# TensorE in source order in the tails, and the last joint projection token tile by token tile

## The chip, the cores and the metric

The kernel runs on one core of a Trainium2 chip. The metric is the device time of one execution in microseconds (us). The median of three runs before the change is 2194.53 us (2194.24 to 2195.38). TensorE, VectorE, ScalarE, GpSimd and SyncE are written PE, DVE, ACT, POOL and SP in the profile's rows. SP issues the loads of weights.

## What is computed

A backbone of two layers over 256 latent tokens and 256 context tokens of width 1024. Each layer is a half-step SwiGLU FFN, a mixer and a second half-step FFN; every one of the three normalises its input, shifts and scales it, and adds its normalised and gated output to the stream:

```python
def rmsnorm(x, w):
    xf = x.astype(jnp.float32)
    y = xf * lax.rsqrt(jnp.mean(xf * xf, axis=-1, keepdims=True) + EPS)
    return (y * w.astype(jnp.float32)).astype(x.dtype)

def modulate(x, g, shift, scale):
    return rmsnorm(x, g) * (1.0 + scale) + shift

def add_residual(x, y, g_post, gate, weight):
    return x + weight * gate * rmsnorm(y, g_post)

def swiglu(h, w_in, w_out):
    a, b = jnp.split(h @ w_in, 2, axis=-1)
    return (jax.nn.silu(a) * b) @ w_out

def branch_merge(ret_out, diff_out, gates, w_out):
    g_a, g_b = jnp.split(jax.nn.sigmoid(gates), 2, axis=-1)
    return (g_a * ret_out + g_b * diff_out) @ w_out
```

The mixer is a retention branch and a differential-attention branch from one input projection; `branch_merge` is its joint output projection. In the last layer only the latent tokens need an output, so the last joint projection and the last FFN work on 256 tokens. The FFN's inner width is 2816.

## The kernel before

The stream lies in SBUF as four token tiles X[0] to X[3] of 128 tokens x 1024, 0 and 1 latent, 2 and 3 context. Every product is taken three times (`mm3`, L330 to L332) on operands split into a hi and a lo part. Weights come from HBM in pieces of 512 KB (`load`, L147), through four raw buffers; `split` writes the hi part on ScalarE (L154) and the lo part on VectorE (L155), into five `w` buffers. Smaller operands live in a ring of twenty slots (`slot`, "r" in the rows), VectorE's scratch in `t` tiles.

An FFN has 22 steps of the first product (`fin_mm`: 128 gate and 128 value columns over eight k), each followed by SiLU and a product, and then the second product over 11 pairs of hidden tiles. In the last FFN, a step of the first product is 48 matmuls of 256 columns.

An FFN and a joint projection end in a **tail**. The first pairs or pieces are worked off for all token tiles; what is left is done one token tile after the other, 12 matmuls for each half of 512 columns, so 24 a tile. Behind a tile's second half `post_norm(t)` follows: two Squares with a sum on ScalarE (L317), the products with the gate row on VectorE (L319), the reciprocal root in three steps on GpSimd (`rstd_2`, L254 to L257) and the residual steps on VectorE (L325). After token tile 1 `after()` is called: `norm_pair(LAT)` normalises X[0] and X[1] (`norm_xn`: L267 on ScalarE, `rstd_2`, L270 on VectorE), transposes them on TensorE (16 transposes, L280), scales and shifts them on ScalarE (eight times L289) and splits them into `h` on VectorE (L292, L293), for the first product of the next stage. The scheduler chooses where in TensorE's order those transposes stand, as for everything. There are four tails with four token tiles: the FFN and the mixer of layer 0, its second FFN and the first FFN of layer 1.

In the last layer the **last joint** has two token tiles. `wide(9)` and `wide(7)` are the last parts of the input projection; `ev_gA(1)` merges the branches (tanh on ScalarE L852, two steps on VectorE L853 and L854, four transposes L861 a token tile, copied and split at L863 and L864) into `M[0, t]` and `M[1, t]`. Then three of the four `wout` pairs are worked off for both tiles as they come, the last for each tile apart, and `norm_pair(LAT)` and the last FFN follow. Loads of `cc` and `wada` (L163, L170) feed the gate rows and have been placed between the others on SP's queue.

Of the kernel before, what the change touches and what calls it, by code (L numbers as in the profile page):

```python
# [12 lines left out]
F32R = mybir.dt.float32r  # L13
# [5 lines left out]
P = 128  # L19
# [15 lines left out]
def build(ctx, tc, a):  # L35
# [84 lines left out]
    def small(n, tag):  # L120
        return sm.tile([P, n], F32, tag=tag, name=tag)
# [125 lines left out]
    def chain(*gs):  # L247
        for g in gs:
            for _ in g:
                yield  # L250

    def rstd_2(ss):
        m = small(2, "pm")
        pool.tensor_scalar(out=m[:, 0:1], in0=ss[:, 0:1], scalar1=1.0 / D, scalar2=EPS, op0=ALU.mult, op1=ALU.add)  # L254
        pool.tensor_scalar(out=m[:, 1:2], in0=ss[:, 1:2], scalar1=1.0 / D, scalar2=m[:, 0:1], op0=ALU.mult, op1=ALU.add)
        r = small(1, "pr")
        pool.tensor_tensor(out=r, in0=m[:, 1:2], in1=cneg[:, 0:1], op=ALU.pow)  # L257
        return r

    def norm_xn(c, alloc):  # L260
        xs = []
        for j in range(2):
            t = 2 * c + j
            ss = small(2, "ss")
            for hf in range(2):
                junk = jp.tile([P, 512], BF16, tag="ja", name="ja")
                act(junk, X[t][:, hf * 512:(hf + 1) * 512], AF.Square, accum_out=ss[:, hf:hf + 1])  # L267
            r = rstd_2(ss)
            xn = alloc([P, D])
            dve.tensor_scalar(out=xn, in0=X[t], scalar1=r, scalar2=None, op0=ALU.mult)  # L270
            xs.append(xn)
        return xs

    def norm_t(c, q, xs):
        bk = bank()
# [30 lines left out]
    def start(AB):  # L306
        h = new_h()
        norm_pair(LAT, AB, h)
        return h, None

    def post_norm(t, yb, Gb, out=None):
        c = t // 2
        ss = small(2, "ss")
        us = []
        for hf in range(2):
            junk = jp.tile([P, 512], BF16, tag="ja", name="ja")
            act(junk, yb[hf], AF.Square, accum_out=ss[:, hf:hf + 1])  # L317
            u = tmp2()
            dve.tensor_tensor(out=u, in0=yb[hf], in1=Gb[c][:, hf * 512:(hf + 1) * 512], op=ALU.mult)  # L319
            us.append(u)  # L320
            banks.put(yb[hf])
        r = rstd_2(ss)
        for hf in range(2):
            xs = X[t][:, hf * 512:(hf + 1) * 512]
            dve.scalar_tensor_tensor(out=xs, in0=us[hf], scalar=r, in1=xs, op0=ALU.mult, op1=ALU.add)  # L325
            if out is not None:
                nc.sync.dma_start(out[t][:, hf * 512:(hf + 1) * 512], xs)

    def mm3(o, wH, wL, xH, xL, start, stop):
        mm(o, lhsT=wH, rhs=xH, start=start, stop=False)  # L330
        mm(o, lhsT=wH, rhs=xL, start=False, stop=False)  # L331
        mm(o, lhsT=wL, rhs=xH, start=False, stop=stop)  # L332

    early = {}
# [18 lines left out]
    def ffn(l, i, st, AB, fetch, pairs, side, nside, after=None, out=None):  # L353
        h, begun = st

        def fin_mm(fs, ws, abs_, c0, c1):
# [11 lines left out]
            banks.put(*ab)  # L368

        f0 = 0  # L370
        if begun is not None:
            f0 = len(begun)
            for f in range(f0):
                fin_ev(f, begun[f])
        elif len(pairs) == 2:
            w01 = [fin_w(l, i, 0), fin_w(l, i, 1)]
            ab01 = [[bank(), bank()], [bank(), bank()]]
            fin_mm((0, 1), w01, ab01, 0, 256)
            xs = norm_xn(CTX, tmp4)
# [14 lines left out]
            done[1] = want  # L394

        for f in range(f0, NF):
            w = fin_w(l, i, f, pin=len(pairs) == 1 and f < 2)
# [36 lines left out]
            pass  # L434
        slots.put(*cs.values())
        cs.clear()
        tail = [fout_w(NP - 2), fout_w(NP - 1)]
        if i == 1 and l < L - 1:
            fin_early(l + 1, 0, ((0, 0),))
        Gb = fetch()  # L440
        for t in range(NT):
            for hf in range(2):
                for e in range(2):
                    for j in range(2):
                        fout_mm(t, j, tail[e][0], tail[e][1], False, e == 1 and j == 1, (hf,))
            post_norm(t, y[t], Gb, out)
            if t == 1 and after is not None:
                after()
        slots.put(*tail[0][1], *tail[1][1], *Gb.values())

    def mixer(l, st, AB, fetch, after):
        h = st[0]
        last = l == L - 1
        lam_init = 0.8 - 0.6 * math.exp(-0.3 * l)
# [519 lines left out]
        fin_early(l, 1, ((0, 0), (0, 1), (1, 0))[:1 if NQ == 2 else 3])  # L974
        Gb = fetch()
        for t in range(NT):
            for hf in range(2):
                for k in range(2 * n0, 8):
                    wo_mm(t, k, w[k - 2 * n0], False, k == 7, (hf,))
            post_norm(t, yb[t], Gb)  # L980
            if t == 1:
                after()
        slots.put(*M.values(), *Gb.values())

    def startup():
        A = small(16, "adaA").rearrange("p (c k) -> p c k", c=2)
# [97 lines left out]
        nc.sync.dma_start(dtab, a["dtab"])  # L1084
        return AB, (h, abs_)

    AB, st0 = startup()
    box = [st0]
    for l in range(L):
        last = l == L - 1  # L1090
        g0, F0 = ada_gate(l, 0, 0.5)
        gs1, AB1 = ada_shsc(l, 1)
        g1, F1 = ada_gate(l, 1, 1.0)
        gs2, AB2 = ada_shsc(l, 2)
        ffn(l, 0, box.pop(), AB, F0, (LAT, CTX), chain(g0, gs1, g1, gs2), 24,
            after=lambda: box.append(start(AB1)))
        mixer(l, box.pop(), AB1, F1, after=lambda: box.append(start(AB2)))
        g2, F2 = ada_gate(l, 2, 0.5)
        if last:
            ffn(l, 1, box.pop(), AB2, F2, (LAT,), g2, 5, out=a["out"])  # L1100
        else:
            gs, AB = ada_shsc(l + 1, 0)
            ffn(l, 1, box.pop(), AB2, F2, (LAT, CTX), chain(g2, gs), 13, after=lambda: box.append(start(AB)))


def rope_tables():
# [64 lines left out]
```

## Time and profile before

| | |
|---|---|
| median of three runs | 2194.53 us (2194.24 to 2195.38) |
| the profiled execution | 2194.1 us, its span 2192.3 us |
| mean granted TensorE clock | 0.996 |
| TensorE busy | 2140.4 us, 98% |
| VectorE, ScalarE, GpSimd busy | 1365.7, 865.8, 129.1 us |
| DMA | 306.99 MB, mean 140 GB/s |

A matmul of 512 columns shows as 0.39 us, but one starts every 0.227 us, since they overlap in the array. So an idle time in brackets counts from the end that is drawn for the matmul before, and a loss is better read from starts. The granted clock is a share of 2.4 GHz; 0.50 is 1.2 GHz.

### The profile page before, as it was taken

Reading aid. Unit: us, or ns where it says so; the run is one execution under the profiler, and the core shown is the slowest. Engines: PE = TensorE matmul, PEld = TensorE weight load, DVE = VectorE, ACT = ScalarE, POOL = GpSimd, SP = SyncE. Lnnn points to the kernel's source line nnn. Section 1 sums busy time; section 2 is a strip of 40 time slices with the busy share of each in tenths; the row PEclk is TensorE's granted clock in tenths of the full one; section 3 lists DMA queues with packets and bytes.
Section 4 is the critical chain, followed back from the end, with each engine's and each line's share of the span. In section 5 each row is a group of like instructions: output and inputs, shape, how many; then the busy total and the mean of one; then the engine's idle time right before and its main releaser. Section 6 shows DMA issues by size and latency. Waiting matters only on the chain. (4 is left out here: it accounts for less than half of the span.)

```text
span 2192.3 us, 27590 instructions
## 1 busy us (share of the span) xinstructions
PE 2140.4 (98%) x10730; PEld 1790.6 (82%) x10730; DVE 1365.7 (62%) x2108; ACT 865.8 (39%) x1367; POOL 129.1 (6%) x236
## 2 busy tenths in 40 slices
PE   7999999999999999999999999999999999998998
PEld 5888888778788878888888888888878888878997
DVE  4799372678665774596243279825347776787554
ACT  3322332553533553522232242223245544565453
POOL 1000000201010000200000010000010000001000
PEclk9999999999999999999999999999999999999999
DMA  8866342222122234364334247734323323355554
GB/s 332 284 218 217 106 135 96 88 68 85 51 91 98 68 97 148 132 211 155 97 124 139 91 161 224 269 96 134 97 67 109 115 93 108 123 194 174 187 183 134
DMA packets 85060, 306.99 MB, mean 140 GB/s; under 512 B 9968, under 2 KB 10048, under 8 KB 84928
## 3 DMA queue, kind: packets, MB, share of 16 engines
q1 hardware_dynamic: 81936, 296.78, 41.2%
q0 software_dynamic: 2848, 8.43, 1.4%
q8 instruction: 84, 1.38, 0.3%
q14 instruction: 48, 0.39, 0.1%
q10 hardware_dynamic: 144, 0.01, 0.0%
HBM read 304.10 MB, written 1.09 MB: 139 GB/s over the span
## 5 line engine op out<-in xcount | busy, mean ns | idle before, releaser
L155 DVE TENSOR_TENSOR w<-raw,w 128x1024 fp32r<-128x1024 f32 x408 | 497.2, 1222 | 465.6 <-ACT w L154 461.9
L154 ACT CAST w<-raw 128x1024 fp32r<-128x1024 f32 x408 | 427.5, 1053 | 665.4 <-PE ps L332 609.3
L330 PE MATMUL ps<-h,w 128*128 128x512 f32 (+1 forms) x1868 | 664.7, 357 | 4.7 <-ACT w L154 2.6
L331 PE MATMUL ps<-h,w 128*128 128x512 f32 (+1 forms) x1868 | 664.9, 356 | 0.4 <-DVE h L293 0.3
L332 PE MATMUL ps<-h,w 128*128 128x512 f32 (+1 forms) x1868 | 663.6, 356 | 1.2 <-DVE w L155 1.2
L330 PEld LDWEIGHTS ps<-h,w 128*128 128x128 f32 x1868 | 353.4, 190 | 57.2 <-DVE h L292 4.7
L332 PEld LDWEIGHTS ps<-h,w 128*128 128x128 f32 x1868 | 353.8, 190 | 50.6 <-DVE w L155 1.8
L331 PEld LDWEIGHTS ps<-h,w 128*128 128x128 f32 x1868 | 354.1, 190 | 50.2 <-DVE h L293 1.4
L174 DVE CUSTOM_DVE_ANT_0 jd<-r,r 128x1024 bf16<-128x1024 f32 x224 | 273.4, 1221 | 6.8 <-DMA r<-wada_dram 2.0
L330 PE MATMUL ps<-w,h 128*128 128x512 f32 x544 | 216.1, 398 | 15.5 <-ACT r L577 11.9
L331 PE MATMUL ps<-w,h 128*128 128x512 f32 x544 | 214.3, 394 | 0.0
L332 PE MATMUL ps<-w,h 128*128 128x512 f32 x544 | 213.8, 394 | 0.0
L330 PE MATMUL ps<-w,gs 128*128 128x512 f32 x504 | 196.2, 389 | 0.0
L331 PE MATMUL ps<-w,gs 128*128 128x512 f32 x504 | 196.1, 389 | 0.0
L332 PE MATMUL ps<-w,gs 128*128 128x512 f32 x504 | 196.1, 389 | 0.0
L366 ACT ACTIVATE t<-ps 128x512 f32<-128x512 f32 (+1 forms) x88 | 47.9, 545 | 252.0 <-PE ps L332 250.6
L330 PEld LDWEIGHTS ps<-w,h 128*128 128x128 f32 x544 | 102.7, 189 | 38.2 <-ACT r L577 15.2
L367 DVE TENSOR_TENSOR r<-ps,t 128x512 f32<-128x512 f32 (+1 forms) x88 | 54.8, 622 | 105.3 <-PE ps L332 77.7
L331 PEld LDWEIGHTS ps<-w,h 128*128 128x128 f32 x544 | 102.8, 189 | 20.2 <-DVE w L155 1.5
L332 PEld LDWEIGHTS ps<-w,h 128*128 128x128 f32 x544 | 102.5, 188 | 20.4
L330 PEld LDWEIGHTS ps<-w,gs 128*128 128x128 f32 x504 | 94.6, 188 | 19.8
L332 PEld LDWEIGHTS ps<-w,gs 128*128 128x128 f32 x504 | 94.6, 188 | 19.6
(180 smaller groups left out, 2132.8 us busy)
## 6 DMA issues: line engine op xcount, KB each, us to landing
raw<-fin_dram SPq DMA_DIRECT2D x176, 512.0 KB, 4.3
r<-wada_dram SPq DMA_DIRECT2D x144, 512.0 KB, 5.1
raw<-fout_dram SPq DMA_DIRECT2D x88, 512.0 KB, 3.6
raw<-winW_dram SPq DMA_DIRECT2D x80, 512.0 KB, 3.6
raw<-winT_dram SPq DMA_DIRECT2D x48, 512.0 KB, 3.6
raw<-wout_dram SPq DMA_DIRECT2D x16, 512.0 KB, 5.6
r<-scr POOLq DMA_DIRECT2D x10, 512.0 KB, 5.4
r<-cc_dram SPq DMA_DIRECT2D x7, 512.0 KB, 5.2
```

Source lines behind the costliest of these rows:

```text
L154: keep(nc.scalar.copy(w[:, 0, :], src))
L155: keep(dve.tensor_tensor(out=w[:, 1, :], in0=src, in1=w[:, 0, :], op=ALU.subtract))
L174: dve.tensor_tensor_reduce(out=junk, in0=r[j], in1=cs[c], scale=1.0, scalar=0.0, op0=ALU.mult, op1=ALU.add, accum_out=out[:, c, 2 * u + j: ...
L330: mm(o, lhsT=wH, rhs=xH, start=start, stop=False)
L331: mm(o, lhsT=wH, rhs=xL, start=False, stop=False)
L332: mm(o, lhsT=wL, rhs=xH, start=False, stop=stop)
L366: act(sg[:, :N], ab[0][:, :N], AF.Silu)
L367: dve.tensor_tensor(out=g[f // 2][:, f % 2, :N], in0=ab[1][:, :N], in1=sg[:, :N], op=ALU.mult)
```

## The change

It has three parts. **Tails**: a function `tail` puts TensorE in source order (`manual_schedule`), and in the source the latent transposes now stand between the two halves of token tile 3; the normed tiles are made by `norm_x` right behind `post_norm` of tiles 0 and 1. **Last joint**: `last_joint` loads and splits all eight `wout` pieces at the start (four into the slot ring by `split2`, four into `w`), does token tile 0 completely, then tile 1, with the norm of tile 0 (`norm_tile`) inside; `head(0)` does three FFN steps for tile 0 alone while the norm of tile 1 is made, and `head(1)` the same for tile 1. Its products have the tokens as stationary operand, so six transposes bring the gated tiles into the FFN's layout; the FFN then starts with its fourth step. `cc` and `wada` loads come later on SP's queue, as slots are short. **Norms**: `rstd_2` takes one GpSimd step less (the Square is scaled by 1/32, so the two sums are added in one step), and the norm of the input is one Square over 1024 columns.

```diff
     def rstd_2(ss):
-        m = small(2, "pm")
-        pool.tensor_scalar(out=m[:, 0:1], in0=ss[:, 0:1], scalar1=1.0 / D, scalar2=EPS, op0=ALU.mult, op1=ALU.add)
-        pool.tensor_scalar(out=m[:, 1:2], in0=ss[:, 1:2], scalar1=1.0 / D, scalar2=m[:, 0:1], op0=ALU.mult, op1=ALU.add)
+        m = small(1, "pm")
+        pool.tensor_scalar(out=m, in0=ss[:, 0:1], scalar1=ss[:, 1:2], scalar2=EPS, op0=ALU.add, op1=ALU.add)
...
+    def norm_x(t, alloc):
+        ss = small(1, "sx")
+        junk = jp.tile([P, D], BF16, tag="ja", name="ja")
+        act(junk, X[t], AF.Square, scale=1.0 / 32, accum_out=ss)
...
+    def tail(NT, part, finish, AB):
+        xs = []
+        with tc.manual_schedule(engines={nc.tensor.engine}):
+            for t in range(NT):
+                part(t, 0)
+                if t == 3 and AB is not None:
+                    h = new_h()
+                    for q in range(4):
+                        norm_q(LAT, q, xs, AB, h)
+                part(t, 1)
+                finish(t)
+                if t < 2 and AB is not None:
+                    xs.append(norm_x(t, tmp4))
+        return None if AB is None else (h, None)
...
+    def last_joint(l, M, fetch, AB):
+        low, high, fw, owned = [], [], [], []
+        for u in range(4):
+            for r in load(a["wout"][l, u]):
+                if u < 2:
+                    wv, w = split2(r)
+                    low.append(wv)
+                    owned += w
+                else:
+                    w = split(r)
+                    high.append([w[:, 0], w[:, 1]])
...
+        for f in range(2):
+            for j in range(2):
+                fw_tile(f, j, f == 0 and j == 0)
+        Gb = fetch()
...
+        with tc.manual_schedule(engines={nc.tensor.engine}):
             for hf in range(2):
+                part(0, range(8), hf)
+            post_norm(0, yb[0], Gb)
+            xs = [norm_x(0, tmp4)]
+            for hf in range(2):
+                part(1, range(4), hf)
+            slots.put(*owned)
+            for j in range(2):
+                fw_tile(2, j, False)
+            part(1, range(4, 8), 0)
+            norm_tile(0, xs[0], AB, h)
+            part(1, range(4, 8), 1)
+            post_norm(1, yb[1], Gb)
+            xs.append(norm_x(1, tmp4))
+            fb = [bank() for _ in range(3)]
+            head(0)
+            norm_tile(1, xs[1], AB, h)
+            head(1)
...
+            for t in range(2):
+                nc.tensor.transpose(tb[:, t * P:(t + 1) * P], sg[:, t], ident)
+            dve.tensor_copy(g[f // 2][:, f % 2, 0:256], tb[:, 0:256])
...
         f0 = 0
-        if begun is not None:
+        if isinstance(begun, dict):
+            g.update(begun)
+            f0 = 3
+        elif begun is not None:
...
+        if last:
+            return last_joint(l, M, fetch, nxt)
```

The order of TensorE in the first tail, before (`t_2782` and `t_2794` are the normed tiles 0 and 1; `r_2662`, `r_2663`, `r_2678` and `r_2679` the hidden tiles of the last two pairs, so that twelve rows of `w,r` are one half of a token tile):

```order
L332 MATMUL ps<-w,r_2662 128x512
L330 MATMUL ps<-w,r_2663 128x512
L280 MATMUL ps<-ident,t_2782 128x128 x4
L331 MATMUL ps<-w,r_2663 128x512
L332 MATMUL ps<-w,r_2663 128x512
L330 MATMUL ps<-w,r_2678 128x512
L280 MATMUL ps<-ident,t_2794 128x128
L280 MATMUL ps<-ident,t_2782 128x128
```

and after it (`t_2724` and `t_2772` are the normed tiles, `r_2667` and `r_2650` the last and the first of the four hidden tiles):

```order
L340 MATMUL ps<-w,r_2667 128x512
L341 MATMUL ps<-w,r_2667 128x512
L342 MATMUL ps<-w,r_2667 128x512
L280 MATMUL ps<-ident,t_2724 128x128
L280 MATMUL ps<-ident,t_2772 128x128
...
L340 MATMUL ps<-w,r_2650 128x512
L341 MATMUL ps<-w,r_2650 128x512
```

Before, the transposes stood in pieces four matmuls into the second half of token tile 2, that is 16 matmuls behind the end of token tile 1; now all 16 stand behind the first half of token tile 3, 36 matmuls behind that end.

The order of ScalarE ahead of the last joint, before (L852 is the tanh of the gate, `t_14797` and `t_14832` the two latent token tiles of its second half, L863 the copy of a merged tile, L154 the casts of `wout` and `fin` pieces):

```order
L820 ACTIVATE r_14724<-ps 128x512
L154 CAST w<-raw 128x1024
L852 ACTIVATE t_14797<-ps 128x512
L154 CAST w<-raw 128x1024 x3
L852 ACTIVATE t_14832<-ps 128x512
L863 CAST r_14829<-ps 128x512
```

and after it (L941 is the former L820, L973 the former L852, L984 the former L863; L347 casts the first four `wout` pieces, L154 the other four):

```order
L941 ACTIVATE r_14660<-ps 128x512
L347 CAST r_14799<-raw 128x1024
L154 CAST w<-raw 128x1024
L973 ACTIVATE t_14733<-ps 128x512
L154 CAST w<-raw 128x1024 x3
L973 ACTIVATE t_14768<-ps 128x512
L984 CAST r_14765<-ps 128x512
```

The number of casts between the two gate activations is the same, but they are those of the sixth to the eighth `wout` piece now, and were those of the second to the fourth before; the other four stood behind the activation of `t_14832`.

The order of TensorE there, after (`t_14768` is the merged tile M[1, 1] ahead of its transposes, `r_14574` the transposed M[0, 0], `r_14765` M[1, 0]):

```order
L982 MATMUL ps<-ident,t_14733 128x128 x4
L340 MATMUL ps<-r_14783,r_14574 128x512
...
L341 MATMUL ps<-w,r_14765 128x512
L342 MATMUL ps<-w,r_14765 128x512
L982 MATMUL ps<-ident,t_14768 128x128 x4
L340 MATMUL ps<-w,r_14765 128x512
```

The transposes of M[1, 1] stood after 11 matmuls of the joint before, of pieces for both token tiles; now after 18, which are the first six pieces of token tile 0.

## Rows read from the trace of the kernel before

**Rows 1.** The page: engines' busy time, and the two costliest groups of instructions.

```profile
PE 2140.4 (98%) x10730; PEld 1790.6 (82%) x10730; DVE 1365.7 (62%) x2108; ACT 865.8 (39%) x1367; POOL 129.1 (6%) x236
...
L155 DVE TENSOR_TENSOR w<-raw,w 128x1024 fp32r<-128x1024 f32 x408 | 497.2, 1222 | 465.6 <-ACT w L154 461.9
L154 ACT CAST w<-raw 128x1024 fp32r<-128x1024 f32 x408 | 427.5, 1053 | 665.4 <-PE ps L332 609.3
```

**Rows 2.** Waits of PE: us in total, times, longest us.

```profile
PE ps L280 <- DVE t L270: 12.7, 10, 4.9
```

**Rows 3.** Timeline of PE, first tail: start us, us, instruction, [idle before <-releaser].

```profile
389.12 0.39 PE L330 MATMUL ps<-w,r 128*128 128x512 f32 x1
390.80 0.65 PE L280 MATMUL ps<-ident,t 128*128 128x128 f32 x4 [1.29 <-DVE t L270]
391.21 0.48 PE L331 MATMUL ps<-w,r 128*128 128x512 f32 x1
...
392.63 1.53 PE L280 MATMUL ps<-ident,t 128*128 128x128 f32 x12 [0.48 <-DVE t L270]
393.92 0.48 PE L331 MATMUL ps<-w,r 128*128 128x512 f32 x1
```

**Rows 4.** Timeline of PE, third tail.

```profile
1258.85 0.39 PE L330 MATMUL ps<-w,r 128*128 128x512 f32 x1
1260.52 0.66 PE L280 MATMUL ps<-ident,t 128*128 128x128 f32 x4 [1.29 <-DVE t L270]
...
1262.36 2.75 PE L280 MATMUL ps<-ident,t 128*128 128x128 f32 x12 [0.48 <-DVE t L270]
1264.77 0.78 PE L331 MATMUL ps<-w,r 128*128 128x512 f32 x1
```

**Rows 5.** Groups by line and form, 380 to 401: busy us, mean ns | idle before.

```profile
L319 DVE TENSOR_TENSOR t<-ps,r 128x512 f32<-128x512 f32 x6 | 4.1, 688 | 4.3 <-ACT ja L317 4.3
L289 ACT ACTIVATE t<-ps,adaB,adaA 128x256 f32<-128x256 f32 x8 | 3.8, 572 | 2.4 <-PE ps L280 2.4
L317 ACT ACTIVATE ja<-ps 128x512 bf16<-128x512 f32 x6 | 3.6, 602 | 6.8 <-PE ps L332 6.7
...
L293 DVE TENSOR_TENSOR h<-t,h 128x512 fp32r<-128x512 f32 x4 | 2.7, 687 | 0.1
...
L292 DVE CAST h<-t 128x512 fp32r<-128x512 f32 x4 | 1.7, 423 | 1.7 <-ACT t L289 1.7
```

**Rows 6.** Timeline of PE, the last joint to the last FFN.

```profile
1965.44 0.48 PE L330 MATMUL ps<-w,r 128*128 128x512 f32 x1
...
1968.16 0.50 PE L330 MATMUL ps<-w,r 128*128 128x512 f32 x1 [0.40 <-DVE r L864]
...
1988.32 0.39 PE L332 MATMUL ps<-w,r 128*128 128x512 f32 x1
1993.63 1.11 PE L280 MATMUL ps<-ident,t 128*128 128x128 f32 x4 [4.92 <-DVE t L270]
1995.47 2.82 PE L280 MATMUL ps<-ident,t 128*128 128x128 f32 x12 [0.72 <-DVE t L270]
1997.94 1.23 PE L330 MATMUL ps<-h,w 128*128 128x256 f32 x4
...
1999.92 0.28 PE L331 MATMUL ps<-h,w 128*128 128x256 f32 x1
```

**Rows 7.** Windows, last FFN: us, busy of PE, PEld, DVE, ACT, POOL, PEclk, DMA, GB/s.

```profile
2040.00:2120.00 80.00, 80.00 (x669) 80.00 (x668) 40.49 (x43) 34.35 (x44) 0.00 (x0) 1.00 0.58 184
```

**Rows 8.** Timelines of DVE and POOL, the norm chain behind the last joint.

```profile
1990.61 1.41 DVE L325 SCALAR_TENSOR_TENSOR X<-t,pr,X 128x512 f32<-128x512 f32 x2
...
1990.66 0.75 POOL L254 TENSOR_SCALAR pm<-ss 128x1 f32<-128x1 f32 x1
...
1993.72 0.27 POOL L255 TENSOR_SCALAR pm<-ss,pm 128x1 f32<-128x1 f32 x1
```

**Rows 9.** DMA issues, 1957 to 1970: KB each, median us to landing.

```profile
raw<-wout_dram SPq DMA_DIRECT2D x5, 512.0 KB, 6.2
```

More of the change, by code (lines that the diff above doesn't have):

```diff
@@ L252, in rstd_2 @@
     def rstd_2(ss):
-        m = small(2, "pm")
-        pool.tensor_scalar(out=m[:, 0:1], in0=ss[:, 0:1], scalar1=1.0 / D, scalar2=EPS, op0=ALU.mult, op1=ALU.add)
-        pool.tensor_scalar(out=m[:, 1:2], in0=ss[:, 1:2], scalar1=1.0 / D, scalar2=m[:, 0:1], op0=ALU.mult, op1=ALU.add)
+        m = small(1, "pm")
+        pool.tensor_scalar(out=m, in0=ss[:, 0:1], scalar1=ss[:, 1:2], scalar2=EPS, op0=ALU.add, op1=ALU.add)
         r = small(1, "pr")
-        pool.tensor_tensor(out=r, in0=m[:, 1:2], in1=cneg[:, 0:1], op=ALU.pow)
+        pool.tensor_tensor(out=r, in0=m, in1=cneg[:, 0:1], op=ALU.pow)
         return r
-    def norm_xn(c, alloc):
[L261 to L272, printed above, removed]
+    def norm_x(t, alloc):
+        ss = small(1, "sx")
+        junk = jp.tile([P, D], BF16, tag="ja", name="ja")
+        act(junk, X[t], AF.Square, scale=1.0 / 32, accum_out=ss)
+        m = small(1, "pm")
+        pool.tensor_scalar(out=m, in0=ss, scalar1=EPS, scalar2=None, op0=ALU.add)
+        r = small(1, "pr")
+        pool.tensor_tensor(out=r, in0=m, in1=cneg[:, 0:1], op=ALU.pow)
+        xn = alloc([P, D])
+        dve.tensor_scalar(out=xn, in0=X[t], scalar1=r, scalar2=None, op0=ALU.mult)
+        return xn
+    def norm_xn(c, alloc):
+        return [norm_x(2 * c + j, alloc) for j in range(2)]
     def norm_t(c, q, xs):
@@ L315, in post_norm @@
         for hf in range(2):
-            junk = jp.tile([P, 512], BF16, tag="ja", name="ja")
-            act(junk, yb[hf], AF.Square, accum_out=ss[:, hf:hf + 1])
+            junk = jp.tile([P, D], BF16, tag="ja", name="ja")
+            act(junk[:, 0:512], yb[hf], AF.Square, scale=1.0 / 32, accum_out=ss[:, hf:hf + 1])
             u = tmp2()
@@ L332, in mm3, with split2, norm_tile @@
         mm(o, lhsT=wL, rhs=xH, start=False, stop=stop)
+    def split2(src):
+        w = [slot([P, 2, 512], F32R) for _ in range(2)]
+        wv = [z.rearrange("p a n -> p (a n)") for z in w]
+        nc.scalar.copy(wv[0], src)
+        dve.tensor_tensor(out=wv[1], in0=src, in1=wv[0], op=ALU.subtract)
+        return wv, w
+    def norm_tile(t, xn, AB, h):
+        A, B = AB
+        ts = slice(t * P, (t + 1) * P)
+        for q2 in range(2):
+            bk = bank()
+            b = bk.rearrange("p (k n) -> p k n", k=4)
+            for kk in range(4):
+                k = 4 * q2 + kk
+                nc.tensor.transpose(b[:, kk], xn[:, k * P:(k + 1) * P], ident)
+            hf = tmp2([P, 4, P])
+            for kk in range(4):
+                k = 4 * q2 + kk
+                act(hf[:, kk, :], b[:, kk], AF.Identity, bias=B[:, t // 2, k:k + 1], scale=A[:, t // 2, k:k + 1])
+            banks.put(bk)
+            for q in (2 * q2, 2 * q2 + 1):
+                hv = hf[:, 2 * (q % 2):2 * (q % 2) + 2]
+                hH = h[q][:, :, 0, ts]
+                dve.tensor_copy(hH, hv)
+                dve.tensor_tensor(out=h[q][:, :, 1, ts], in0=hv, in1=hH, op=ALU.subtract)
     early = {}
@@ L351, in fin_part, with ffn @@
                         h[k // 2][:, k % 2, 1, c0:c1], fresh and k == 0, k == KD - 1)
-    def ffn(l, i, st, AB, fetch, pairs, side, nside, after=None, out=None):
+    def ffn(l, i, st, AB, fetch, pairs, side, nside, nxt=None, out=None):
         h, begun = st
@@ L396, in ffn @@
         for f in range(f0, NF):
-            w = fin_w(l, i, f, pin=len(pairs) == 1 and f < 2)
+            w = fin_w(l, i, f, pin=False)
             ab = [bank(), bank()]
@@ L436, in ffn @@
         cs.clear()
-        tail = [fout_w(NP - 2), fout_w(NP - 1)]
+        last2 = [fout_w(NP - 2), fout_w(NP - 1)]
         if i == 1 and l < L - 1:
@@ L440, in ffn, with part @@
         Gb = fetch()
-        for t in range(NT):
-            for hf in range(2):
[L443 to L451, printed above, removed]
+        def part(t, hf):
+            for e in range(2):
+                for j in range(2):
+                    fout_mm(t, j, last2[e][0], last2[e][1], False, e == 1 and j == 1, (hf,))
@@ L452, in mixer @@
+    def mixer(l, st, AB, fetch, nxt):
         h = st[0]
@@ L973, in mixer, with part @@
         w = sum((wo_w(u) for u in range(n0, 4)), [])
-        fin_early(l, 1, ((0, 0), (0, 1), (1, 0))[:1 if NQ == 2 else 3])
+        fin_early(l, 1, ((0, 0),))
         Gb = fetch()
[L976 to L982, printed above, removed]
+        def part(t, hf):
+            for k in range(2 * n0, 8):
+                wo_mm(t, k, w[k - 2 * n0], False, k == 7, (hf,))
+        st = tail(NT, part, lambda t: post_norm(t, yb[t], Gb), nxt)
         slots.put(*M.values(), *Gb.values())
+        return st
     def startup():
```

60 lines of the change are left out of this document (49 added, 11 removed).

## Prediction

> **What bounds the kernel now.** I read the page first. TensorE is busy for 98% of the span [rows 1], so some 50 us at most can come out of its idle time, and a change that removes no matmul gains only where TensorE stands still or runs at its low clock. The list of TensorE's waits comes next: the transposes of the norm (L280) waited for the normed tile (L270, on VectorE) 12.7 us in 10 waits, the longest 4.9 [rows 2]. It is the largest entry of that list, and it is the one that this change is about. The TensorE timeline shows where those waits lie: two short ones in each of the four tails, 1.29 and 0.48 in the first [rows 3] and the same pair in the third [rows 4], and 4.92 + 0.72 at the end of the last joint [rows 6].
>
> The profiled execution took 2194.1 us, its span 2192.3; the median of the runs is 2194.53. All sums start from 2194.1. About 0.2%, or 4.4 us, is what a measurement of this kernel can tell from no change.
>
> **The four tails: what goes.** In the first tail the matmul ahead of the transposes starts at 389.12 and the first one behind all 16 of them at 393.92 [rows 3]: 4.80 us. The work in between is 0.23 for that matmul, 0.41 for four transposes (390.80 to 391.21), 0.77 for the three matmuls behind them and 1.29 for twelve more (392.63 to 393.92): 2.7. So 2.1 are lost. The second and the fourth tail show the same two waits. In the third, the same stretch takes 5.92 (1258.85 to 1264.77): there the twelve transposes alone take 2.4 [rows 4], since the clock fell; 3.2 lost, 1.1 of it by the clock. Sum: 3 x 2.1 + 3.2 = **9.5 us that can go**. In source order the transposes stand 36 instead of 16 matmuls behind the end of token tile 1 (first order excerpts), 20 x 0.227 = 4.5 us later. The normed tile came 3.5 us after the place of the first ones (389.12 to 392.63), so it is there 1 us early.
>
> **The four tails: what is late next.** Count from T, the end of token tile 3's first half. TensorE does 16 transposes (1.7) and 12 matmuls (2.7) and is at the next stage at T + 4.4. ScalarE does one Square, 0.60 and 0.2 for its read, then eight normed copies, 3.76 in all [rows 5], done at T + 4.55; the first cast of a weight piece, 1.05 [rows 1], at T + 5.6. VectorE does hi and lo of the first two quarters, 2 x (0.42 + 0.69) [rows 5], from T + 1.75 to T + 4.0; the third's hi, a product 0.69, the third's lo and the fourth's hi, to T + 6.2; then the lo half of the weight piece, 1.22 [rows 1], to T + 7.4. TensorE wants this piece 10 matmuls into the stage, at T + 6.8: 0.6 of waiting. The next piece stands behind one lo, one product, two residual steps (1.41, [rows 8]) and its own 1.22: T + 11.4, wanted 16 matmuls on at T + 11.0: 0.4. With 0.1 for ScalarE's last copy **1.1 us come back in each tail**; I take 1.0, as the pieces of tails two and three are FFN pieces wanted a little later: 4.0 in all. Net: 9.5 - 4.0 = **5.5**. Bounds: 9.5 if nothing comes back, 1.1 (the third tail's clock) if both waits do.
>
> **The last joint.** Its first matmul starts at 1965.44, its last at 1988.32; then the whole norm chain of tile 1 stands bare, the transposes come at 1993.63 and 1995.47, and the FFN begins at 1997.94 with a low clock: nine matmuls of 256 columns take 1.98 [rows 6], later ones 80 / 669 = 0.120 each [rows 7], so 0.9 is lost there. Three FFN steps are 144 such matmuls, 17.2, and the fourth step starts at 1997.94 + 17.2 + 0.9 = **2016.1**. After, the same stretch is 96 matmuls of 0.227 (21.8), 20 transposes (2.1), 144 of 0.120 (17.2) and six transposes more for the gated tiles (0.7): 41.8, from 1965.4 to 2007.2 without a wait. I add three:
> - The lo half of merged tile M[1,0]: 0.4 before [rows 6], 0.5 after.
> - The transposes of M[1,1]. They stand after 18 matmuls, at about 1970. ScalarE has the cast of the eighth w_out piece ahead of the gate's activation for that token tile (second excerpts). That piece can load only once the fourth piece has left its buffer, behind VectorE's end of the attention, about 1961; w_out took 6.2 from issue to landing there [rows 9], and I take 5.5, as the wada loads that shared the stretch are moved away. Then cast 1.05, lo 1.22, three steps of 0.69 and one more lo between them: ready at 1971.6 (1970 to 1973), a wait of 1.6 (0 to 3).
> - Tile 1's head. Its norm chain, bare for 4.9 before, now runs beside the 72 matmuls of head(0), 8.6 us, but has VectorE's splits of 1.22 ahead of it in two places: 8 to 8.5. Then four transposes, two copies, hi and lo come before the first matmul of head(1): 1.2 (0.5 to 1.9).
>
> Together 3.3: the fourth step starts at 2010.5, **5.6 earlier**. Bounds: 8.9 with no wait, 1.3 with both waits at their upper ends and a fall of the clock behind each (rival 2).
>
> **At nothing.** One Square and one GpSimd step less in each norm: in the tails TensorE now arrives after the normed tile, and at the start and the end of the program the last step of the chain keeps its place; without that cover a GpSimd step is worth 0.27 to 0.75 [rows 8]. On SP's queue one cc load and six of wada, 512 KB each, move from ahead of and among the w_out loads to behind the loads of the three FFN steps. They feed the gate that the last norm wants 150 us later; if one held up a fin load, about its landing of 6 us would show.
>
> **Sum.** 2194.1 - 5.5 - 5.6 = **2183.0**.
>
> **Rivals.**
> 1. *The tails' wait only moves.* ScalarE and VectorE, not the order of TensorE, set when the next stage can go on. For it: both end within a microsecond of TensorE in the sum above. Against: only 0.6 and 0.4 come out of it. Gains 1.1 and 5.6: 2187.4. Chance 0.14.
> 2. *The last joint gives its gain back through waits and the clock.* After 4.92 of idling the clock was low [rows 6]; after 1.29 it stayed up in the first tail [rows 3] and fell in the third, at a price of 1.1 [rows 4]. So the two waits may bring it down as well: 2.1 more of waiting and 2 x 1.1 leave a gain of 1.3, and the time is 2187.3. Chance 0.14.
> 3. *GpSimd is held off by VectorE.* A one-column GpSimd step took 0.75 at 1990.66, when VectorE had just begun two residual steps, and 0.27 at 1993.72, when VectorE stood still [rows 8]. Tile 1's chain has four such steps, now beside splits of 1.22. Each could grow by 0.95, and 0.3 of that is covered by head(0): 3.5 more, 2186.5. Chance 0.10. The Trainium skill's page "SBUF — State Buffer", section "SBUF: two separate sides", has the rule: VectorE with two SBUF inputs and GpSimd share a port pair, whichever starts first holds it for its whole instruction, and the other blocks. By that rule, the trace agrees (0.75 beside VectorE, 0.27 alone).
> 4. *Slower: the ring of w_out loads.* All eight pieces are now wanted before 1970, instead of spread up to 1988, with four load buffers, and the activation behind each cast waits along with it on ScalarE. Lateness counts twice, since the eighth piece takes the fourth's buffer. The 11.1 us are gone when both land 5.6 later than I took them, at 11 instead of 5.5 us. At 14 each the time is 2183 + 17 = 2200. For it: w_out already took 6.2 in a stretch in which TensorE wanted less of it [rows 9]. Against: that is its median there, and the wada loads leave. Chance 0.04.
> 5. *Nothing.* The fixed order makes TensorE wait elsewhere for as much: 2194. Chance 0.05.
> 6. *More.* None of the new waits comes: 2194.1 - 9.5 - 8.9 = 2175.7. Chance 0.10.
>
> **How the numbers follow.** The forecast has 0.43, with a range of its own of 2180 to 2186. Rivals 1 to 3 with the bounds of the joint's waits carry the range up to 2190, half of rival 6 down to 2176; left out are 4, 5, the rest of 6, and 1 and 2 together, under 0.2. Slower by over 0.2% is rival 4, 0.04; within it are rival 5 and rivals 1 and 2 together, 0.08; faster is the rest, 0.88.
>
> **What would show it.** In each tail TensorE's waits for the normed tile are gone, and waits of 0.4 to 0.6 for the lo half of a weight piece stand within 12 us behind. In the last joint the 4.92 is gone, a wait of 1 to 2 stands ahead of M[1,1]'s transposes and one of about 1 ahead of head(1). It is wrong if TensorE waits over 2 us behind each tail or over 4 for M[1,1], or if the clock is low in the head.

## The result, and the profile after

The change takes **2182.44 us** (median of four runs, 2180.43 to 2185.12), beside 2194.39 for the kernel before: a ratio of 0.9946, 95% interval 0.9929 to 0.9963. It was run again later, as experiment 10: 2183.67 (2179.82 to 2185.38, five runs), ratio 0.9945 [0.9932, 0.9957]. The profiled execution is the slowest of the first four, 2185.12, with a span of 2183.3.

The page of the change, the lines that answer to [rows 1]:

```profile
PE 2140.8 (98%) x10736; PEld 1792.6 (82%) x10736; DVE 1364.9 (63%) x2119; ACT 859.4 (39%) x1331; POOL 108.8 (5%) x194
```

TensorE is as busy as before and the span is 9.0 shorter, so it is idle time that went. The list of TensorE's waits has no entry for the normed tile any more, and these three are new:

```profile
PE ps L982 <- DVE t L975: 2.0, 1, 2.0
PE ps L341 <- DVE w L155: 1.0, 1, 1.0
PE ps L340 <- DVE h L368: 0.8, 1, 0.8
```

So the 12.7 us of [rows 2] (L280) are gone. In each of the four tails TensorE now does its transposes in one go; the fourth, on TensorE:

```profile
1627.14 0.39 PE L342 MATMUL ps<-w,r 128*128 128x512 f32 x1
1627.38 1.91 PE L280 MATMUL ps<-ident,t 128*128 128x128 f32 x16
1629.04 0.48 PE L340 MATMUL ps<-w,r 128*128 128x512 f32 x1
...
1633.22 0.39 PE L340 MATMUL ps<-w,h 128*128 128x512 f32 x1
1634.57 0.50 PE L341 MATMUL ps<-w,h 128*128 128x512 f32 x1 [0.96 <-DVE w L155]
...
1646.30 0.50 PE L340 MATMUL ps<-w,h 128*128 128x512 f32 x1 [0.31 <-DVE h L292]
```

All 16 transposes follow without a gap (1.66 from start to start); what comes back comes behind them, as a wait of 0.96 for the lo half of a weight piece. VectorE's timeline there shows why this half is late:

```profile
1632.36 0.68 DVE L293 TENSOR_TENSOR h<-t,h 128x512 fp32r<-128x512 f32 x1
1632.96 0.42 DVE L292 CAST h<-t 128x512 fp32r<-128x512 f32 x1
1633.29 1.22 DVE L155 TENSOR_TENSOR w<-raw,w 128x1024 fp32r<-128x1024 f32 x1
```

Counted from T = 1627.38, where the transposes begin, it ends at T + 7.1, behind hidden splits and a product. The prediction had T + 7.4, and TensorE wanting it at T + 6.8; it wanted it seven matmuls into the stage and not ten, at T + 6.1.

The last joint, TensorE. Against [rows 6], the 4.92 and 0.72 are gone, and two waits of the three that were predicted are there:

```profile
1959.75 0.48 PE L340 MATMUL ps<-r,r 128*128 128x512 f32 x1
...
1966.17 0.66 PE L982 MATMUL ps<-ident,t 128*128 128x128 f32 x4 [2.05 <-DVE t L975]
...
1986.92 0.28 PE L340 MATMUL ps<-w,h 128*128 128x256 f32 x1
...
1995.56 1.03 PE L359 MATMUL ps<-ident,t 128*128 128x128 f32 x8
1997.39 0.38 PE L340 MATMUL ps<-w,h 128*128 128x256 f32 x1 [0.79 <-DVE h L368]
```

VectorE ahead of these transposes, in the same execution: the gate's product for M[1,1], the lo half of the first fin piece after 1.24 of idle, the merge's last step.

```profile
1962.37 0.68 DVE L974 SCALAR_TENSOR_TENSOR t<-t,r 128x512 f32<-128x512 f32 x1
1964.29 1.22 DVE L155 TENSOR_TENSOR w<-raw,w 128x1024 fp32r<-128x1024 f32 x1 [1.24 <-ACT w L154]
1965.43 0.68 DVE L975 TENSOR_TENSOR t<-t,r 128x512 f32<-128x512 f32 x1
```

Behind TensorE's wait of 2.05 the clock was low. The windows (columns as in [rows 7]; the clock is the figure behind POOL's) give 0.50 at 1968 to 1970, which is 1.2 GHz:

```profile
1966.00:1968.00 2.00, 1.83 (x9) 1.58 (x10) 1.92 (x3) 1.76 (x3) 0.00 (x0) 0.88 0.96 322
1968.00:1970.00 2.00, 2.00 (x6) 1.55 (x5) 2.00 (x3) 1.41 (x3) 0.00 (x0) 0.50 0.96 330
1970.00:1972.00 2.00, 2.00 (x8) 1.58 (x8) 0.88 (x2) 1.05 (x1) 0.00 (x0) 0.76 0.99 346
```

**Where the 9.0 us of the profiled execution are.** Setting the start of one and the same matmul in both traces side by side gives the shift up to there:

| stretch | before to the change, profiled | the change run again |
|---|---|---|
| start, to the first tail | +2.0 | -0.7 |
| four tails, with what follows each | -8.5 | -8.6 |
| from there to the last joint (before: 1924 to 1965) | +0.8 | +0.9 |
| last joint to last FFN | -3.4 | -5.9 |
| span | -9.0 | -14.3 |

The first and the third row are mostly the clock. In windows of 10 us from 20 to 40 it was 0.73 and 0.83 in the first trace of the change, 0.87 and 1.00 in the second, 0.83 and 1.00 before; from 1905 to 1935 it was 0.89 in both and 0.94 before, and the two long waits that lie there were no longer than before (3.16 and 0.82 in the first trace, 3.21 and 0.95 before). The program of the two traces of the change is one and the same, so the first row differs from run to run. One profile alone would have given -9.0 or -14.3 for the same kernel; the medians say -12.0 and -11.3.

### The profile page after: what moved, and what is told of

Its sections match the earlier page's. It is cut to its first block, busy times and chain, and to the rows that moved or that the text cites. A ratio compares the mean times of both kernels' runs of the same rounds, so it can differ in the third digit from the quotient of the medians.

```text
span 2183.3 us, 27485 instructions
## 1 busy us (share of the span) xinstructions
PE 2140.8 (98%) x10736; PEld 1792.6 (82%) x10736; DVE 1364.9 (63%) x2119; ACT 859.4 (39%) x1331; POOL 108.8 (5%) x194
## 5 line engine op out<-in xcount | busy, mean ns | idle before, releaser
L155 DVE TENSOR_TENSOR w<-raw,w 128x1024 fp32r<-128x1024 f32 x399 | 486.2, 1222 | 456.0 <-ACT w L154 452.9
L154 ACT CAST w<-raw 128x1024 fp32r<-128x1024 f32 x399 | 419.1, 1055 | 660.7 <-PE ps L342 598.2
L340 PE MATMUL ps<-h,w 128*128 128x512 f32 (+1 forms) x1820 | 652.7, 359 | 5.1 <-ACT w L154 3.0
L341 PE MATMUL ps<-h,w 128*128 128x512 f32 (+1 forms) x1820 | 652.2, 359 | 0.4 <-DVE h L293 0.3
L342 PE MATMUL ps<-h,w 128*128 128x512 f32 (+1 forms) x1820 | 651.4, 358 | 0.6 <-DVE w L155 0.6
L340 PEld LDWEIGHTS ps<-h,w 128*128 128x128 f32 x1820 | 345.2, 190 | 58.4 <-DVE h L292 4.6
L342 PEld LDWEIGHTS ps<-h,w 128*128 128x128 f32 x1820 | 345.7, 190 | 50.1 <-DVE w L155 1.3
L341 PEld LDWEIGHTS ps<-h,w 128*128 128x128 f32 x1820 | 345.7, 190 | 49.9 <-DVE h L293 1.4
L340 PE MATMUL ps<-w,h 128*128 128x512 f32 (+1 forms) x552 | 219.0, 398 | 16.3 <-ACT r L698 11.7
L341 PE MATMUL ps<-w,h 128*128 128x512 f32 (+1 forms) x552 | 216.8, 393 | 1.0 <-DVE w L155 1.0
L342 PE MATMUL ps<-w,h 128*128 128x512 f32 (+1 forms) x552 | 216.8, 393 | 0.0
L340 PEld LDWEIGHTS ps<-w,h 128*128 128x128 f32 x552 | 104.4, 189 | 39.8 <-ACT r L698 15.1
L341 PEld LDWEIGHTS ps<-w,h 128*128 128x128 f32 x552 | 104.4, 189 | 21.1 <-DVE w L155 2.3
L342 PEld LDWEIGHTS ps<-w,h 128*128 128x128 f32 x552 | 104.3, 189 | 20.9 <-DVE h L293 0.4
```

What stands on the lines that cost most here:

```text
L154: keep(nc.scalar.copy(w[:, 0, :], src))
L155: keep(dve.tensor_tensor(out=w[:, 1, :], in0=src, in1=w[:, 0, :], op=ALU.subtract))
```

## The experiments

Eleven runs were made, each beside the kernel before. What Theory 1, Theory 2 and the rivals are, each expectation says for itself. Where a gain is given by stretches, it comes from the starts of one and the same matmul in two traces, as in the table above.

**1. The tails (and the norms), with the old last joint.**

```diff
-        if last:
-            return last_joint(l, M, fetch, nxt)
+        if last:
+            for t in range(NT):
+                part(t, 0)
...
+            norm_pair(LAT, nxt, h2)
```

The loads of the first FFN pieces are as before, too.

> The tails and the norms of the change, with the last joint of before (three w_out pairs for both tiles, norm of both tiles behind it). Theory 1, read from the trace after the change: the four tails are 2.05, 2.26, 3.87 and 2.24 us shorter and give back 0.3, 0.25, 0.25 and 1.25 in the stages behind them, 8.3 in all, and the shorter norm chain takes about 1 off the bare chain of the last joint, so about 9 us faster than before, 2185.4. Theory 2, the prediction's sum: 5.5 from the tails, 2188.9. Rival 1 of the prediction (the wait only moves): about 1 us, 2193. In all of them the waits of the transposes for the normed tile are gone in the tails and the long one, 4.9 before, is about 4 at the last joint.

Measured 2188.0 (2185.88 to 2188.62), ratio 0.9967 [0.9955, 0.998]: 7.0 gained. The time is 2.6 above Theory 1's and 0.9 under Theory 2's, but the stretches are not Theory 2's: in the trace the four tails with what follows them gain 8.8, 1.1 go again ahead of the last joint, and the joint gains 0.1, where Theory 1 had about 1. The tails' waits for the normed tile are gone as in the change; what is left is the last joint's, 4.55 and 1.15, no less than the 4.92 and 0.72 of [rows 6].

```profile
PE ps L280 <- DVE t L268: 5.7, 2, 4.6
```

**2. The last joint (and the norms), with the old tails.**

```diff
     def tail(NT, part, finish, AB):
-        with tc.manual_schedule(engines={nc.tensor.engine}):
-            for t in range(NT):
-                part(t, 0)
...
+            if t == 1 and AB is not None:
+                h = new_h()
+                norm_pair(LAT, AB, h)
```

> The last joint and the norms of the change, with TensorE's order in the four tails left to the scheduler as before. Theory 1, from the trace: the last joint gains 3.4 net of its new wait of 2.05 for the transposes of M[1,1] and of a low clock behind it, and the shorter norm chain, which is bare in the tails' old order, takes up to 0.7 off each of the four tails, so 4 to 6 us faster than before, about 2189.4. Theory 2, the prediction's sum: 5.6 from the joint and nothing from the norms, 2188.8. Apart from the time they differ in the tails' waits: unchanged at 1.8 per tail by theory 2, about 1.1 by theory 1.

Measured 2185.36 (2184.05 to 2189.17), ratio 0.9962 [0.995, 0.9975]: 9.6 gained, more than either theory gave. Two things are in it. TensorE waited 1.04 for M[1,1] here and the clock stayed at 1.00, so the joint gained 6.0 in the trace. And the shorter norms cut the tails' waits to 1.1 a tail, as Theory 1 had it; with the clock, which no longer fell in the third tail, the tails gained 4.1 (experiment 4).

**3. One VectorE instruction moved: the lo half of the first fin piece behind the last merge step.** This takes the lo half out from between the two merge steps shown above.

```diff
             if keep:
-                w = split(r)
+                with tc.issue_after(merged[1, 1].ins): w = split(r)
```

> The change with one instruction moved: on VectorE the lo half of the first FFN piece comes behind the last step of the merge for M[1,1], instead of between its two steps; TensorE's order is the same. Theory 1: the wait of 2.05 ahead of M[1,1]'s transposes was VectorE standing at that lo half, whose load had not landed; it goes to 0 to 0.3, the clock stays up behind it, and the time falls by 2 to 3.5 against the change, to 2179 to 2180.5. Theory 2, as the prediction put it: the cast of the eighth w_out piece ahead of the gate's activation sets it; the lo half took only its own 1.22, so 0.8 or more of the wait stays and the gain is about 1.2.

Measured 2183.03 (2180.96 to 2183.74), ratio 0.9944 [0.9932, 0.9957]: nothing that can be told from the change. The wait for M[1,1] is gone, and 1.23 for M[1,0] is there instead. M[1,1] itself was ready no earlier, 6.39 behind the first joint matmul, where it was 6.36 in the change. ScalarE shows a second cause: the cast of the eighth w_out piece waited 3.99 for its landing, and the gate's activation and the copy of M[1,0] stood behind it.

```profile
1961.86 1.05 ACT L154 CAST w<-raw 128x1024 fp32r<-128x1024 f32 x1 [3.99 <-DMA raw<-wout_dram]
1962.81 0.59 ACT L975 ACTIVATE t<-ps 128x512 f32<-128x512 f32 x1
1963.30 0.58 ACT L986 CAST r<-ps 128x512 fp32r<-128x512 f32 x1
```

So there are two pieces whose landing holds work that doesn't need them, and this run alone can't say which of them decided in the change. The issue lists do. The eighth w_out piece was issued some 4 us ahead of the first joint matmul in every trace with the new joint. Its time to landing, in the change and here:

```profile
raw<-wout_dram SPq DMA_DIRECT2D x1, 512.0 KB, 3.6
```

```profile
raw<-wout_dram SPq DMA_DIRECT2D x1, 512.0 KB, 5.9
```

It took 3.6 to 3.9 in the six traces in which no split was moved (both of the change, experiments 2, 5, 6 and 9) and 5.8 to 6.1 in the four with splits moved behind (3, 7, 8 and 11). In the change its cast had started when the joint began, and the fin piece decided (experiments 10 and 11); with the edit that takes the fin piece out of the way, the w_out piece landed 2.3 later. Why it did is not shown.

**4. The kernel before, with the shorter norms alone.**

```diff
-        pool.tensor_scalar(out=m[:, 0:1], in0=ss[:, 0:1], scalar1=1.0 / D, scalar2=EPS, op0=ALU.mult, op1=ALU.add)
-        pool.tensor_scalar(out=m[:, 1:2], in0=ss[:, 1:2], scalar1=1.0 / D, scalar2=m[:, 0:1], op0=ALU.mult, op1=ALU.add)
+        pool.tensor_scalar(out=m, in0=ss[:, 0:1], scalar1=ss[:, 1:2], scalar2=EPS, op0=ALU.add, op1=ALU.add)
...
+        act(junk, X[t], AF.Square, scale=1.0 / 32, accum_out=ss)
```

> Before with only the shorter norms: one GpSimd step less in each reciprocal root, one Square over 1024 columns instead of two over 512. Theory 1: in the tails of before TensorE waits for this chain, so each of the four loses 0.5 to 0.8 of its 1.8 of waiting and the last joint about 1 of its 5.6: 3 to 4 us faster, about 2191. Theory 2 (the prediction's term at nothing, if it held for the kernel of before too): within 1 us of before.

Measured 2191.84 (2189.46 to 2193.34), ratio 0.9985 [0.9976, 0.9994]: 3.1 gained, as Theory 1 said. Where TensorE waits for the chain, a step less is time: the pair of waits in a tail fell from 1.29 + 0.48 to 0.92 + 0.21. Behind the shorter pair the clock stayed up in the third tail, too (the twelve transposes took 1.53, and 2.75 before), and this tail alone gained 2.2 in the trace. At the last joint the waits fell by only 0.26 (to 4.55 + 0.83), where about 1 was expected.

**5. The change, with the longer norms back.**

```diff
-        m = small(1, "pm")
-        pool.tensor_scalar(out=m, in0=ss[:, 0:1], scalar1=ss[:, 1:2], scalar2=EPS, op0=ALU.add, op1=ALU.add)
+        m = small(2, "pm")
+        pool.tensor_scalar(out=m[:, 0:1], in0=ss[:, 0:1], scalar1=1.0 / D, scalar2=EPS, op0=ALU.mult, op1=ALU.add)
...
-        act(junk, X[t], AF.Square, scale=1.0 / 32, accum_out=ss)
...
+            act(junk, X[t][:, hf * 512:(hf + 1) * 512], AF.Square, accum_out=ss[:, hf:hf + 1])
```

> The change with the longer norms of before (three GpSimd steps, two Squares for the input norm). Theory 1 (the new order covers the norm chain, so its length is worth nothing there): no wait for the normed tile in the tails, 182.4 +- 1 over 2000 as the change has, that is 2182.4 (2181.5 to 2183.5); in the last joint the xn of tile 1 was ready 0.3 before TensorE came, so a GpSimd step of 0.3 to 0.7 more there may show as a wait of 0 to 0.7. Theory 2 (the shorter norms are worth the same 3.1 as they were alone in the old order): 2185.5, with waits of TensorE for the normed tile in the tails.

Measured 2182.33 (2180.94 to 2186.93), ratio 0.9945 [0.9933, 0.9957], no difference from the change. The same edit was worth 3.1 in the old order and nothing that can be told in the new one. Experiments 1, 2 and 4 fit with it: 7.0 + 9.6, less the 3.1 that the shorter norms bring where an old order is left, is 13.5, and all together brought 12.0; each of the intervals is some 2.7 us wide to either side.

**6. The transposes in the tails six matmuls earlier.** This asks whether the time that comes back behind the tails comes from the place of the transposes or from VectorE's queue.

```diff
                 if t == 3 and AB is not None:
+                    part(t, 0, 0)
                     h = new_h()
...
+                    part(t, 0, 1)
```

> The change, with the latent transposes of the four tails six matmuls earlier (in the middle of token tile 3's first half, 1.36 us). Theory 1 (the 2.15 that come back behind the tails are VectorE's and ScalarE's work behind the transposes, which ends too late): the waits behind tail 4 (0.96 and 0.31) shrink to under 0.3, 0.25 in the other stages go, no wait for the normed tile appears: 1.5 to 2 faster than the change, 2180.5 to 2181. Rival (the products of token tile 3 then come behind the hidden splits on VectorE and its whole queue shifts, so that the wait goes to the next weight piece): the waits keep their sum within 0.5, 2182 to 2182.5. Rival 2 (the normed tile is not there yet): waits of 0.3 or more for it in the tails, 2183 to 2185.

Measured 2183.78 (2181.61 to 2186.4), ratio 0.9948 [0.9935, 0.996]: no gain. The rival named the right thing, the wait for the next weight piece, though not its size: in the fourth tail that wait fell from 0.96 to 0.59, but the stages behind the other three tails got one of 0.53 to 0.59 that they did not have. By the starts of the matmuls 2.8 came back behind the tails instead of 1.8. No wait for the normed tile appeared. The reason is in the timeline of VectorE: the hidden splits begin at 1628.85, right behind the residual steps of token tile 2, and from there it has no gap up to the weight piece.

```profile
1627.53 1.41 DVE L338 SCALAR_TENSOR_TENSOR X<-t,pr,X 128x512 f32<-128x512 f32 x2
1628.85 0.42 DVE L292 CAST h<-t 128x512 fp32r<-128x512 f32 x1
...
1633.57 1.22 DVE L155 TENSOR_TENSOR w<-raw,w 128x1024 fp32r<-128x1024 f32 x1
```

**7. Both splits of the last joint moved behind, and M[1,1]'s transposes after 24 matmuls.**

```diff
+                    with tc.issue_after(merged[1, 1].ins), tc.issue_after(tanhs[1, 1].ins), tc.issue_after(copies[1, 0].ins):
+                        w = split(r)
...
-                w = split(r)
+                with tc.issue_after(merged[1, 1].ins): w = split(r)
...
-            for hf in range(2):
-                part(0, range(8), hf)
+            part(0, range(8), 0)
+            flush()
+            part(0, range(8), 1)
```

> The change, and in the last joint: the transposes of M[1,1] stand behind the first half of token tile 0 (24 matmuls instead of 18), and the split of the eighth w_out piece and of the first fin piece are issued behind the gate's activation, the copy of M[1,0] and the last merge step. Theory 1 (the wait ahead of M[1,1]'s transposes and the fall of the clock behind it cost 3 to 4 there, and come from those two splits standing in front on ScalarE and VectorE): no wait of over 0.3 at M[1,0] and M[1,1], the clock stays up behind, the FFN's fourth step starts 2 to 3.5 earlier than in the change: 2179 to 2180.5. Theory 2 (the eighth piece lands so late that its product waits for it instead): a wait of 0.5 to 2 at the eighth piece's matmuls, and no gain of over 1: 2181.5 to 2182.5.

Measured 2181.19 (2179.19 to 2181.81), ratio 0.9934 [0.9922, 0.9946]. Neither wait is there, the clock is 1.00 from 1955 to 1985, and no wait for the eighth piece came, so Theory 2's sign is missing. With 1.3 less than the change's first median the time misses Theory 1's 2179 to 2180.5 by 0.7, and the intervals of the two ratios overlap.

**8. That joint with the tails of experiment 6.**

> The last joint of the run with the eighth piece behind, and the tails of the run with the transposes six matmuls earlier, together. Theory 1: their gains add, 3.5 to 5.5 faster than the change: 2177 to 2179. Rival (what is gained at either place is lost to the clock or to the next wait): within 1 of the change, 2181.5 to 2183.5.

Measured 2181.63 (2179.86 to 2182.23), ratio 0.9937 [0.9924, 0.9951]. The time is that of experiment 7, and the tails add nothing to it. The rival's bounds take it in only just, and for another reason than it gave.

**9. One call moved: TensorE has nothing beside the norm chain of tile 1.**

```diff
-            head(0)
             norm_tile(1, xs[1], AB, h)
+            head(0)
             head(1)
```

> The change with one call moved: the transposes of tile 1's norm stand ahead of the three FFN steps for tile 0, not behind them, so TensorE has nothing beside the norm chain of tile 1. Theory 1 (what the three steps by token tile bring is that they cover this chain): TensorE waits 4.9 (the bare chain of before) to 8.4 (from the last joint matmul to the normed tile in the change's trace), the clock is low behind it for 0.9 to 1.2, and the wait of 0.8 ahead of tile 1's steps goes: 5 to 8.7 slower than the change, 2187.5 to 2191. Rival (the fin pieces land so late that the steps could not run earlier than they would then): 0 to 2 slower, 2182.5 to 2184.5.

Measured 2191.4 (2189.68 to 2192.38), ratio 0.9982 [0.9973, 0.9992]: 7.7 slower than the change beside it, as Theory 1 had it (5 to 8.7 slower; the time is 0.4 over its range, as the change itself was 1.2 slower there than at first). TensorE stands still for 8.35, and 1.2 GHz follows:

```profile
1992.43 1.94 PE L359 MATMUL ps<-ident,t 128*128 128x128 f32 x8 [8.35 <-DVE t L268]
```

```profile
1990.00:1995.00 5.00, 2.57 (x12) 2.60 (x13) 3.23 (x5) 1.45 (x5) 1.41 (x2) 0.50 0.96 308
1995.00:2000.00 5.00, 5.00 (x32) 5.00 (x31) 2.14 (x7) 1.45 (x5) 0.00 (x0) 0.68 0.29 101
```

Experiment 1 differs from this one in the last joint and its loads, and is 3.4 faster. The intervals of these two just overlap, but the traces agree: from the first joint matmul to the end this run is 3.7 slower than the kernel before, and experiment 1 is 0.1 faster. So doing the last joint token tile by token tile is worse than the old way as long as nothing covers the chain; the three FFN steps by token tile are what makes it pay.

**10 and 11. The change and the kernel of experiment 7 once more, on one chip.**

> The change itself once more, beside the next run on one chip. Theory 1 (the wait ahead of M[1,1]'s transposes depends on when the eighth w_out piece lands, and the clock falls behind it only when it is over 2): 2182.4 +- 1, and where the wait in its profile is under 1.3, no low clock at 1965 to 1975. Rival (the wait of 2.05 and the fall belong to the order): wait of 2 and a low clock again.

> The last joint with the splits of the eighth w_out piece and of the first fin piece moved behind, and M[1,1]'s transposes after 24 matmuls, once more, beside the change on one chip. Theory 1 (1.2 to 3.3 of waiting, plus 1.2 where the clock falls, are gone): 1.3 to 3 faster than the change beside it. Rival (chip and run only): within 0.5 of it.

Measured 2183.67 for the change (given above) and 2181.16 (2178.82 to 2181.97), ratio 0.9934 [0.9921, 0.9946], for the other: 2.5 apart here, 1.3 in the first comparison. The intervals of the two ratios overlap; over all runs of each, nine and ten, the medians are 2182.53 and 2181.18. Its medians are the lowest of all, with experiment 8 (2181.63) too near to be told from it. The trace of the change had a shorter wait for M[1,1] this time, and the full clock behind it:

```profile
1957.03 0.48 PE L340 MATMUL ps<-r,r 128*128 128x512 f32 x1
...
1962.50 0.66 PE L982 MATMUL ps<-ident,t 128*128 128x128 f32 x4 [1.10 <-DVE t L975]
```

```profile
1960.00:1970.00 10.00, 8.90 (x42) 7.11 (x41) 7.12 (x8) 5.75 (x8) 0.63 (x1) 1.00 0.95 318
```

The cast of the first fin piece sets this wait. It started 2.51 behind the first joint matmul here, and 2.70, 3.46 and 4.69 behind it in experiment 5, the first trace of the change and experiment 6; the waits were 1.10, 1.26, 2.05 and 3.27, each 1.41 to 1.44 less than that start. The order of the last joint's instructions around that cast is the same in these four, so the landing of one piece makes the difference. It is not the piece that the expectation named: the cast of the eighth w_out piece started 0.02 to 0.21 ahead of the first joint matmul in all four. ScalarE, the second trace of the change:

```profile
1959.54 1.05 ACT L154 CAST w<-raw 128x1024 fp32r<-128x1024 f32 x1 [0.51 <-DMA raw<-fin_dram]
```

and the first:

```profile
1963.21 1.05 ACT L154 CAST w<-raw 128x1024 fp32r<-128x1024 f32 x1 [1.64 <-DMA raw<-fin_dram]
```

## Why the prediction was right, step by step

The time, 2182.44, stands 0.6 beside the forecast of 2183.0. The waits went where the prediction said, but that the sum came out so near is luck: the tails gained 3.0 more than the sum had, 0.8 went ahead of the last joint, where the sum has nothing, and the joint gained 2.2 less in the first trace. 8.5 - 0.8 + 3.4 is the forecast's 11.1; in the second trace it is 8.6 - 0.9 + 5.9 = 13.6.

- **The tails, what goes: right, a little small.** 10.4 us went where 9.5 were predicted. In the third tail it was 3.87, as the fall of the clock went along with the waits.
- **The tails, what is late next: mechanism right, price twice too high.** The sum gave 1.0 a tail, in two waits, from ScalarE's and VectorE's work behind the transposes. Behind the fourth tail 1.0 came back, in the one wait of 0.96 at the lo half of a weight piece. The second of the two did not come: the 0.31 at 1646.30 stood in the same place before.

```profile
1652.81 0.50 PE L330 MATMUL ps<-w,h 128*128 128x512 f32 x1 [0.29 <-DVE h L292]
```

  Behind the other tails 0.25 to 0.3 came back by the starts of the matmuls, in all about 1.8 instead of 4.0. Of the prediction the step "I take 1.0" failed for three tails out of four: in the FFN stages behind the second and third tail the waits are 0.21 and 0.26, and they were 0.22 and 0.26 before. Net 8.5 instead of 5.5. That VectorE's queue sets it, rather than the place of the transposes, is what experiment 6 showed; rival 1 in the strong form (the wait only moves) did not come.
- **The last joint: 3.4 and 5.9 in two traces, where 5.6 was predicted.** The wait ahead of M[1,1] was there (1.10 and 2.05; predicted 1.6, 0 to 3), that ahead of tile 1's steps too (0.79; predicted 1.2), that for M[1,0] was not (predicted 0.5; 1.23 in experiment 3). The wait for M[1,1] came in its size, but not for the reason given, and added up from its own terms the prediction's M[1,1] is ready at 1972.1, a wait of 2.1 and not 1.6. The prediction had the landing of the eighth w_out piece in front, at 5.5; it took 3.6. The lo half of the fin piece it counted as "one more lo between them", at 1.22 for its work alone. That lo half also waits for its own landing, 1.24 in the first trace, and this decided. The step that failed is to price an instruction in a queue by its duration only, when it waits for a transfer itself.
- **The clock behind the joint's wait was left out of the sum** and put into the lower bound and rival 2. It fell behind waits of 2.05 and 3.27 and stayed up behind 0.72 to 1.26. In the first trace of the change the fall cost 1.6: the shift between its two traces grew by 2.5 over the joint, 0.95 of it the longer wait.
- **Ahead of the last joint the sum has no term.** Both traces of the change lose 0.8 to 0.9 there, with a granted clock of 0.89 from 1905 to 1935, where it was 0.94 before. What lowers it is open.
- **The joint without waits was taken 0.8 too good.** The kernel of experiment 11 has only the 0.79 left and gains 7.3 there, where 8.9 - 0.79 = 8.1 would follow. This was not followed up.
- **At nothing: right, in the new order only.** Experiments 4 and 5 are the two halves: 3.1 without the cover, nothing that can be told with it. In the change the normed tile of tile 1 is ready 0.3 before TensorE comes, so the cover is thin. The moved loads of cc and wada made no wait in the last FFN.
- **Rival 3, GpSimd held off by VectorE: seen, but covered.** In tile 0's chain, with VectorE free, the first step of each norm took 0.29 and 0.22; in tile 1's, beside VectorE's splits, 0.74 and 1.00:

```profile
1976.18 0.29 POOL L254 TENSOR_SCALAR pm<-ss 128x1 f32<-128x1 f32 x1 [12.09 <-ACT ja L327]
...
1979.93 0.22 POOL L264 TENSOR_SCALAR pm<-sx 128x1 f32<-128x1 f32 x1 [2.81 <-ACT ja L262]
...
1988.68 0.74 POOL L254 TENSOR_SCALAR pm<-ss 128x1 f32<-128x1 f32 x1 [7.87 <-ACT ja L327]
...
1992.87 1.00 POOL L264 TENSOR_SCALAR pm<-sx 128x1 f32<-128x1 f32 x1 [2.80 <-ACT ja L262]
```

  Two of four steps grew, by 0.45 and 0.78, and no wait of TensorE came of it. The Trainium skill's page "SBUF — State Buffer", section "SBUF: two separate sides", says that a VectorE instruction with two SBUF inputs holds the port that GpSimd shares until it ends. By that rule, the trace agrees: the step of 1.00 ended at 1993.87, and the two splits beside it at 1993.78.
- **Rival 4, the ring of w_out loads: not seen in the change.** The eight w_out pieces took 4.2 from issue to landing (median), where 6.2 was read in [rows 9] and 5.5 taken; the eighth took 3.6.

The range of 2176 to 2190 held every run of the change. The spread of its nine runs, 5.6, is as wide as the terms of the sum.

## What to carry to other kernels

An operation in TensorE's order is best put where its operand is a little early, and work that needs no late operand behind it: three FFN steps that could start with half of the tokens turned a bare chain of 8.35 us, and a joint 3.7 us slower than the old one, into a gain. When a wait is removed, look at the queues of the engines behind it for an instruction that waits for a transfer: it holds everything after it, whether that needs the transfer or not. And make a shortening of a chain only where something waits for the chain: the same edit was worth 3.1 us before the reordering and nothing after it.

## What was not expected of the hardware

The same kernel's trace had a second stretch of low clock at 30 to 40 us (0.83) in one execution and none in another, and was 2.7 us later by the first tail, 0.4 of it from the first load. Nothing that was run here tells why. Nor does anything tell why the eighth w_out piece landed after 3.6 to 3.9 us in six traces and after 5.8 to 6.1 in the four whose splits stand further behind. In the two traces of the change and those of experiments 5 and 6 a transfer of 512 KB landed up to 2.2 us earlier or later against TensorE's own progress, as the starts of the fin piece's cast show (2.51 to 4.69 behind the same matmul), and with the clock the joint's gain on the kernel before went from 5.9 us to 3.4, and to 2.4 in experiment 6.
